# A batched attention-times-value product: from a scheduled tile program to hand-written engine programs with a register loop on TensorE

## The chip, the cores and the metric

One core of one Trainium2 chip. The metric is the device time of one launch in microseconds (us). Most runs of one kernel agree within 0.1% here. A "span" is the time from the first to the last instruction in the trace, 1.7 to 1.9 us less than the time (in e5 2.5 to 2.8 us). A transfer "lands" when its last piece has arrived, by the trace's semaphore records. Engines: PE is TensorE's matmul, PEld its weight load, DVE is VectorE, ACT ScalarE, POOL GpSimd, SP the sync engine.

## The reference

```python
batch, n_heads, seq, head_dim = 8, 12, 1024, 64
def reference(attn_weights, v):          # (8,12,1024,1024) and (8,12,1024,64), float32
    return np.einsum('bhqs,bhsd->bhqd', attn_weights, v).astype(np.float32)
```

There is no softmax: 403 MB of weights are read once, and every element is used in one product with 64 columns. Heads are taken two at a time, 48 "pairs" of 8 MB each; a pair is worked in 16 blocks, each of 64 queries of both heads.

## The kernel before

It is written on a tile framework that orders instructions and places semaphores. GpSimd issues the weight loads, which cast float32 to bf16 on the way (427.8 MB read at HBM, 240.4 MB in packets). The weights arrive with the query on the partitions, so TensorE transposes them (two bf16 as one 32-bit word; 128x128 f32 in the timeline), DVE and ACT copy the transposed blocks from PSUM to SBUF, and TensorE multiplies. The last three pairs ("direct") use the transposed weights as the stationary operand, in groups of four blocks, and get by without a transpose back.

```python
    abf_pool = ctx.enter_context(tc.tile_pool(name="abf", bufs=2))   # 4 MB of weights each
    at_pool = ctx.enter_context(tc.tile_pool(name="at", bufs=2))
    vr_pool = ctx.enter_context(tc.tile_pool(name="vr", bufs=2))     # v, for two pairs
    ...
    def pair(ip):
        ...
        for g in range(G):
            transpose_g(abf, at, g)              # 16 x 4 transposes, then a copy each
        load_ahead(ip)                           # weights of pair ip+2 into the freed buffer
        for h in range(2):
            for half in range(2):
                multiply(at, vbf, po, h, half)
        to_sbuf(po, ot)
        if ip % 2 == 0 and ip // 2 + 1 < NV:
            spread_v(ip // 2 + 1)                # v of the NEXT two pairs onto all partitions
        for j0 in (0, 4):
            last = transpose_back(ot, o_halves, j0, 4)
        if ip < NP - 1 - HELD:                   # HELD = 7: the last outputs are kept back
            store(ip, osb)
        else:
            held[ip] = osb
    ...
    def load_ahead(ip):
        nxt = ip + 2
        if nxt < NP:
            if nxt % 2 == 1 and (nxt + 1) // 2 < NV:
                load_v((nxt + 1) // 2)           # v of pairs nxt+1 and nxt+2
            last = load_attn(nxt)
            if nxt == NP - 1:
                ...                              # the held stores, behind the last load
```

## Time and profile before

| | before |
|---|---|
| time, median (range) | 1061.45 us (1061.05 to 1061.7, 4 runs) |
| span | 1059.6 us |
| DMA share, 100 to 900 us | 1.01 to 1.02 |
| PE busy / TensorE clock granted | 76% / 0.855 |
| instruction packets on the DMA engines | 44 of 16 KB |

The row to read first is the DMA share, the busy time of the core's 16 DMA engines. At 1.01 to 1.02 I read the idle time of the other engines (PE's 4.3 and 5.0 us ahead of two pairs in the prediction's timeline) as free: only work of the DMA engines, and the two ends of the run, should change the time. The lines themselves stand in the prediction.

### The profile page before, as it was taken

Reading aid. Unit: us, or ns where it says so; the run is one execution under the profiler, and the core shown is the slowest. Engines: PE = TensorE matmul, PEld = TensorE weight load, DVE = VectorE, ACT = ScalarE, POOL = GpSimd, SP = SyncE. Lnnn points to the kernel's source line nnn. Section 1 sums busy time; section 2 is a strip of 40 time slices with the busy share of each in tenths; the row PEclk is TensorE's granted clock in tenths of the full one; section 3 lists DMA queues with packets and bytes.
Section 4 is the critical chain, followed back from the end, with each engine's and each line's share of the span. In section 5 each row is a group of like instructions: output and inputs, shape, how many; then the busy total and the mean of one; then the engine's idle time right before and its main releaser. Section 6 shows DMA issues by size and latency. Waiting matters only on the chain.

```text
span 1059.6 us, 12899 instructions
## 1 busy us (share of the span) xinstructions
PE 808.4 (76%) x5640; PEld 645.0 (61%) x5640; DVE 390.7 (37%) x590; ACT 399.6 (38%) x486; POOL 71.8 (7%) x137
## 2 busy tenths in 40 slices
PE   0988778876778767787687876888678776788996
PEld 0676567654666556665476655766557555676785
DVE  0443334433344333343334333343334333344443
ACT  0353334433344333344344333443334333343542
POOL 2000000000000000000000000000000000001011
PEclk9998878988888888788888887788889887788999
DMA  9999999999999999999999999999999999999998
GB/s 217 219 218 234 222 237 231 225 226 222 239 224 232 222 231 237 223 220 231 238 226 229 227 224 236 229 222 229 229 230 235 221 227 228 236 215 210 217 215 243
DMA packets 19208, 240.43 MB, mean 227 GB/s; under 512 B 2128, under 2 KB 2512, under 8 KB 11984
## 3 DMA queue, kind: packets, MB, share of 16 engines
q0 software_dynamic: 18432, 238.03, 100.0%
q1 hardware_dynamic: 720, 1.57, 0.4%
q8 instruction: 44, 0.72, 0.2%
q14 instruction: 12, 0.10, 0.0%
HBM read 427.82 MB, written 25.17 MB: 428 GB/s over the span
## 4 chain that ended last, share of the span: by engine, by line
DMA 73%; issue 14%; PE 9%; POOL 2%; ACT 1%; DVE 0%; POOLq 0%
DMA abf<-in_attn_weights_dram 73%; PE pt L150 5%; PE px L186 2%; ACT osb L194 1%; POOL vr L124 1%; POOL out_dram L203 1%; PE px L136 1%; PE px L252 1%; PE po L169 0%; DVE vbf L144 0%; POOL abf L108 0%; DVE at L159 0%; ACT at L159 0%; DVE osb L263 0%; ACT osb L263 0%
## 5 line engine op out<-in xcount | busy, mean ns | idle before, releaser
L150 PE MATMUL pt<-ident,abf 128*128 128x128 f32 x3072 | 463.2, 319 | 194.3 <-DMA abf<-in_attn_weights_dram 194.3
L150 PEld LDWEIGHTS pt<-ident,abf 128*128 128x128 f32 x3072 | 449.7, 214 | 209.4 <-issue 116.3
L159 DVE COPY at<-pt 128x1024 bf16<-128x1024 bf16 x480 | 319.5, 688 | 443.1 <-PE pt L150 441.7
L159 ACT COPY at<-pt 128x1024 bf16<-128x1024 bf16 x288 | 288.7, 1012 | 223.3 <-PE pt L150 129.2
L169 PE MATMUL po<-at,vbf 128*64 128x512 bf16 x1440 | 216.5, 391 | 0.0
L169 PEld LDWEIGHTS <-vbf 128*64 128x64 bf16 x1440 | 106.5, 108 | 92.9
L194 ACT COPY osb<-px 128x512 f32<-128x512 f32 x90 | 50.8, 587 | 154.9 <-PE px L186 151.5
L181 ACT COPY ot<-po 128x512 f32<-128x512 f32 x45 | 26.3, 585 | 191.4 <-PE po L169 191.4
L186 PE MATMUL px<-ident,ot 128*128 128x128 f32 x360 | 69.8, 340 | 30.3 <-DVE vbf L144 17.4
L186 PEld LDWEIGHTS px<-ident,ot 128*128 128x128 f32 x360 | 52.8, 174 | 50.7 <-DVE vbf L144 28.7
L144 DVE CAST vbf<-px 128x512 bf16<-128x512 f32 x48 | 33.2, 691 | 95.9 <-PE px L136 95.9
L181 DVE COPY ot<-po 128x512 f32<-128x512 f32 x45 | 31.1, 691 | 100.8 <-PE po L169 100.8
L136 PE MATMUL px<-vr,spread 32*128 32x512 bf16 x384 | 53.8, 386 | 18.5 <-DVE vbf L144 18.5
L108 POOL DMA_DIRECT2D abf<-in_attn_weights_dram x58 | 31.5, 546 | 512.5 <-PE pt L150 507.2
L203 POOL DMA_DIRECT2D out_dram<-osb x47 | 25.2, 536 | 462.8 <-ACT osb L194 424.8
L144 ACT CAST vbf<-px 128x512 bf16<-128x512 f32 x48 | 28.1, 585 | 63.7 <-PE px L136 63.7
L136 PEld LDWEIGHTS <-spread 32*128 32x128 bf16 x384 | 17.2, 93 | 52.5 <-issue 43.0
L252 PE MATMUL px<-vbf,at 128*128 128x128 bf16 x384 | 23.9, 219 | 2.3 <-ACT at L159 1.2
L252 PEld LDWEIGHTS <-at 128*128 128x128 bf16 x384 | 22.5, 98 | 3.1 <-DVE at L159 1.5
L263 ACT COPY osb<-px 64x256 f32<-64x256 f32 (+2 forms) x14 | 4.7, 337 | 20.6 <-DVE osb L263 20.6
L124 POOL DMA_DIRECT2D vr<-in_v_dram x23 | 12.4, 538 | 0.0
L263 DVE COPY osb<-px 64x256 f32<-64x256 f32 (+2 forms) x14 | 5.3, 378 | 18.4 <-PE px L252 18.4
(10 smaller groups left out, 6.1 us busy)
## 6 DMA issues: line engine op xcount, KB each, us to landing
abf<-in_attn_weights_dram POOLq DMA_DIRECT2D x44, 4096.0 KB, 33.2
out_dram<-osb POOLq DMA_DIRECT2D x47, 512.0 KB, 20.0
vr<-in_v_dram POOLq DMA_DIRECT2D x23, 512.0 KB, 21.4
abf<-in_attn_weights_dram POOLq DMA_DIRECT2D x4, 2048.0 KB, 25.6
abf<-in_attn_weights_dram POOLq DMA_DIRECT2D x7, 1024.0 KB, 27.3
v<-in_v_dram SPq DMA_DIRECT2D x1, 1024.0 KB, 4.7
abf<-in_attn_weights_dram POOLq DMA_DIRECT2D x1, 512.0 KB, 29.7
abf<-in_attn_weights_dram POOLq DMA_DIRECT2D x2, 256.0 KB, 30.1
```

Source lines behind the costliest of these rows:

```text
L108: last = nc.gpsimd.dma_start(out=abf[:, ds(g0, gn)].rearrange("p g s -> p (g s)"), in_=attn_p[ip][:, ds(g0 * S, gn * S)],)
L124: nc.gpsimd.dma_start(out=vr.rearrange("p b x -> p (b x)"), in_=v_g[iv])
L136: nc.tensor.matmul(out=px, lhsT=spread[rows, b], rhs=vr[rows, b], start=(b == 0), stop=(b == VB - 1),)
L144: copy(out=vbf[:, :, h % 2], in_=px.rearrange("p (k d) -> p k d", k=SB))
L150: nc.tensor.matmul(out=pt[:, k], lhsT=words[:, k], rhs=ident, is_transpose=True, start=(k == 0), stop=(k == KW - 1),)
L159: copy(out=at[:, g].rearrange("c k j two -> c (k j two)"), in_=pt.rearrange("c k j -> c (k j)").bitcast(bf16),)
L169: nc.tensor.matmul(out=po[h][ds(half * D, D)], lhsT=vbf[:, 2 * kw + par, h], rhs=at[:, ds(half * GH, GH), kw, ds(h * HP, HP), par], start= ...
L181: copy(out=ot[:, :, h], in_=po[h].rearrange("p (j q) -> p j q", j=GH))
L186: last = nc.tensor.matmul(out=px[:, j], lhsT=ot[:, j0 + j].rearrange("p h q -> p (h q)"), rhs=ident, is_transpose=True, start=(j == 0), st ...
L194: nc.scalar.copy(out=o_halves[:, :, ds(j0, jn)].rearrange("p half j d -> p j half d"), in_=px.rearrange("p j (half d) -> p j half d", half=2),
L203: nc.gpsimd.dma_start(out=out_p[ip].rearrange("p g d -> p (g d)"), in_=osb.rearrange("p g d -> p (g d)"), single_packet=True,)
L252: behind = nc.tensor.matmul(out=px[:, g - g0].rearrange("p h d -> p (h d)"), lhsT=at[:, g, kw, :, par], rhs=vbf[:, 2 * kw + par].rearrange ...
```

## The change

The intent is to drop the framework's scheduling: one program per engine with its own semaphores, a loop on TensorE so that its program is short, and the transposes back of a pair moved behind the transposes of the next pair so that TensorE needn't wait for the copies. Core of the diff (about 650 lines; cuts marked):

```diff
-    at_pool = ctx.enter_context(tc.tile_pool(name="at", bufs=2))
-    vr_pool = ctx.enter_context(tc.tile_pool(name="vr", bufs=2))
-    HELD = 7
+    HELD = 9
+    with tc.tile_critical(no_gpsimd_drain=True):
+        at = sb("at", [P, G, KW, P, 2], bf16)                 # one, not two
+        vr = sb("vr", [P, VB, SB * D], bf16)
+        vr_last = sb("vr_last", [P, VB, SB * D], bf16)        # the last block of v alone
...
+        def pe_pair(i, n, before, waits, wait_v, first=False):
+            for g in range(G):
+                if g in waits:
+                    pe.wait_ge(*waits[g])
+                if g >= 4:
+                    pe.wait_ge(s_cp[i][g - 4], n)
+                transpose_g(abf[i], g)
...
+            spread_v(i, vr)                  # this pair's v, no longer the next one's
+            if not first:
+                transpose_back()             # of the pair before
...
+            multiply(i)
+        def pe_direct(p):
...
+                transpose_g(abf[i], g)
+                if g == 3:
...
+                    elif p == NP - 2:
+                        pe.wait_ge(s_vlast, 16)
+                    spread_v(i, vr_of(p))
...
+        with nc.Fori(1, LOOPED // 2, 1, engines=(PE,)) as it:
+            n = pe.snap(it + 1)
+            loaded = pe.snap(it * 16)
+            twice = pe.snap(loaded + 16)
+            pe_pair(0, n, it, {0: (s_abf[0], twice)}, (s_v, loaded))
+            pe_pair(1, n, n, {0: (s_abf[1], twice)}, None)
...
+        for p in range(NP - 2):              # GpSimd
+            pool.wait_ge(s_t[True], (p + 1) * PER_DVE)
+            if p % 2 == 1 and (p + 1) // 2 < NV:
+                iv = (p + 1) // 2
+                if iv < NV - 1:
+                    pool.wait_ge(s_sp[1], p + 1)
+                load_v(iv)
+            load_attn(p + 2)
+            if 0 < p <= HELD_FROM:
+                store(p - 1)
+        for p in range(HELD_FROM, NP - 1):
+            store(p)
```

## The prediction

> **What bounds the kernel now.** I read the busy shares first, then the DMA queues, the chain of work that ended last, and single stretches. From the page of the kernel before:
>
> ```profile
> PE 808.4 (76%) x5640; PEld 645.0 (61%) x5640; DVE 390.7 (37%) x590; ACT 399.6 (38%) x486; POOL 71.8 (7%) x137
> DMA  9999999999999999999999999999999999999998
> q0 software_dynamic: 18432, 238.03, 100.0%
> q8 instruction: 44, 0.72, 0.2%
> HBM read 427.82 MB, written 25.17 MB: 428 GB/s over the span
> DMA 73%; issue 14%; PE 9%; POOL 2%; ACT 1%; DVE 0%; POOLq 0%
> ```
>
> No compute engine is full, but the DMA row is nine in 39 of 40 slices, and the software queue alone fills the time of all 16 DMA engines. The chain is mostly DMA, by line the load of the attention weights (73%). The table of stretches says the same more finely (columns: stretch, its length, busy us and count of PE, PEld, DVE, ACT, POOL, granted clock, DMA share, GB/s):
>
> ```profile
> 300.00:500.00 200.00, 154.93 (x1027) 122.15 (x1024) 73.87 (x110) 75.39 (x91) 12.21 (x23) 0.82 1.02 229
> 500.00:700.00 200.00, 153.31 (x1019) 120.70 (x1017) 72.50 (x109) 75.54 (x92) 11.68 (x22) 0.84 1.01 228
> 1040.00:1050.00 10.00, 8.78 (x111) 8.12 (x109) 4.64 (x9) 3.72 (x6) 1.59 (x3) 1.00 1.03 335
> 1050.00:1060.00 10.00, 1.81 (x21) 1.42 (x20) 1.12 (x3) 1.54 (x4) 0.00 (x0) 0.79 0.41 160
> ```
>
> The share is 1.01 to 1.02 (packets overlap a little) up to the last 10 us. So the question for any change is only whether it alters the work of the DMA engines, or lets their queue run dry. The timeline around one pair answers the second (start, duration, engine, line, operation):
>
> ```profile
> 506.70 9.24 PE L150 MATMUL pt<-ident,abf 128*128 128x128 f32 x64 [4.33 <-DMA abf<-in_attn_weights_dram]
> 515.88 4.81 PE L169 MATMUL po<-at,vbf 128*64 128x512 bf16 x32
> 516.24 0.53 POOL L108 DMA_DIRECT2D abf<-in_attn_weights_dram  x1 [12.36 <-PE pt L150]
> 529.65 0.20 PEld L150 LDWEIGHTS pt<-ident,abf 128*128 128x128 f32 x1 [5.00 <-DMA abf<-in_attn_weights_dram]
> ```
>
> The next load is issued at 516.24, when the 64 transposes have freed its buffer; the load already in the queue lands only at about 529.6. So **13.4 us of work are still queued** when more is added. PE waits 4 to 5 us per pair for data, and that wait costs nothing. A pair takes 21.8 us.
>
> **The small thing that is left.** The chain in order of time gives one landing for every second pair:
>
> ```profile
> 178.69 0.70 PE pt L150 x2
> 222.33 0.70 PE pt L150 x2
> 266.97 0.49 PE pt L150
> 310.57 0.49 PE pt L150
> ```
>
> Steps: 43.64, 44.64, 43.60. Over the whole chain every step is 43.6 except four of about 44.65 (ending at 266.97, 442.45, 661.53, 880.60), 1.05 more. Two pairs move 16.78 MB of weights, 1.05 MB of v and 1.05 MB of output, 18.87 MB. The queue line above has 44 instruction packets, 0.72 MB, 16 KB each. This is TensorE's program: 11,280 instructions (5640 matmuls, 5640 weight loads) of 64 bytes are 0.72 MB. In the trace's list of single packets each fetch takes 0.89 to 0.97 us of one DMA engine, and the durations repeat with a period of eight fetches. In each of the four long steps lies a fetch of the first of these eight classes (0.893 us, or 892), and the long steps lie 4 or 5 double pairs apart, about eight fetches. My reading: fetches go round the DMA engines, and **only the one that falls on the slowest engine delays the landings, by 1.05 us**.
>
> [...] 18.87 MB in 43.6 us are 433 GB/s[...]. No loop is in the kernel before[...]. [...]
>
> **The change part by part.**
>
> (1) Traffic of data: the same loads with the same pieces, the same 4 MB per pair, the same v and output bytes, two weight buffers as before. 0 us.
>
> (2) TensorE's loop: pairs 2 to 43 come from 21 rounds of a body of two pairs. What is left in the program is 2 pairs ahead, 2 in the body, 1 after, 3 direct. A pair has 64 transposes, 16 spreads, 8 transposes back, 32 multiplications: 120 matmuls, 240 instructions; with some 18 waits as instructions of their own 258. A direct pair has 64 + 16 + 128 = 208 matmuls, about 456 with its waits. 5 x 258 + 3 x 456 = 2658 instructions are 10.4, so 11 blocks of 256 instead of 44. The body, 516 instructions, is about 33 KB[...]; I take it that it stays. 33 fetches fewer, one in eight on the slowest engine, 1.05 us each: **minus 4.3 us**.
>
> (3) One branch and a few register operations per round[...], on PE, beside 13.4 us of slack. 0 us.
>
> (4) Own semaphores: the waits on PE become about 18 per pair. Even at 0.2 us exposed for each of the 12 before transposes, the next load would be issued 2.4 us later, and 11 us would still be queued. 0 us. One copy of `at` instead of two, and the spread and transposes back between transposes and multiplication: PE's pair, in the stretches above 16.8 us of a 21.8 us pair (154 of 200 us busy), has the same work in another order; in-order issue makes the single buffer safe without a new wait ahead of the next pair's transposes other than those of the copies. The buffer of the weights still comes free after the transposes, which now come first in a pair as before. 0 us. The load of v waits for one spread in every second pair, some 2 us, ahead of the weights' load: inside the slack.
>
> (5) The end: 9 held stores instead of 7 lie behind the last loads, so the last piece lands some 2.5 us earlier (a 512 KB store at 433 GB/s is 1.2 us), and the last transposes no longer wait for the products before them. But the packets show 4 KB store packets to the very end, on engines that lag the fastest by up to 10 us; the engine that ends last has its whole share to do in any order. The end of the compute chain comes earlier by 2 to 4 us and is covered by stores: 0 us, at best minus 1.
>
> (6) The start: entering one critical section may add a barrier ahead of the first load, which is issued at 1.26 us now, and as the DMA is the bound, that would count fully. Plus 0.4 us, a guess.
>
> Sum: 1061.36 - 4.3 + 0.4 = 1057.5 us.
>
> **The rivals.** (a) *The loop refetches its body each round.* Then 21 rounds x 2 to 3 blocks plus the rest give 60 to 75 fetches, 15 to 30 more than now: plus 2 to 4 us if spread the same way, 1064 to 1066. [...] (b) *TensorE becomes the bound*, since waits on registers are slow or the serial order (transposes, spread, back, wait for the cast, multiply) leaves gaps. PE would need over 13 us more per pair between a landing and its last transpose before the queue dries, or over 21.8 us of work per pair in all, some 5 us more than now; beyond that, each us per pair costs 47 us of span. For it: PE at 76% is the next in line. Against: the 4 to 5 us waits for data. Then 1085 or more. (c) *The scheduling itself was costing much*, as the author's effort suggests: the 14% "issue" and 116 us of PE's weight load waiting on issue would come back. Against: those lie beside a DMA share of 1.01[...]. (d) *Fetches do not matter at all* and the long steps have another cause: 1061.5.
>
> **Range and chances.** The centre is (2) with (6). Below, a better end and every fetch counting give some 1053; above, rival (a) or (d) with a costlier start gives 1062. Faster by over 2% means under 1040[...]: 1%. Slower by over 2% needs rival (b): 3%. Within 2%: 96%.
>
> **What would show it.** Right: instruction packets near 11 on that queue; DMA share still 1.01 in the middle; landings every 43.6 us with at most one or two long steps; PE's wait for the weights still some us in each pair, DVE and ACT busy unchanged. Part (5): PE's last matmul comes earlier against the end, with stores filling the rest. Wrong: 60 or more fetches (rival a); a DMA share under 0.98 in the middle, or landings over 45 us apart with PE waiting on copies or semaphores (rival b); steps below 43.3 us (rival c); 11 fetches but the same long steps (rival d); a first load issued later than 2 us.

Cut from the recorded text are figures and rules that no run of this case shows, and what was argued from them. The sum came to 1057.5 us (1061.36, minus 4.3 of part (2), plus 0.4 of part (6)), and no number of it is cut; only the 0 us of part (3) has lost its ground, the author's estimate for a branch (measured later: 0.21 us in the changed kernel). That the loop's body stays was not shown by the kernel before. Two figures have their ground in the page: 64 bytes an instruction is the 0.72 MB of fetches over 11,280 instructions, and 256 to a block is a packet of 16 KB in such instructions. That TensorE issues in order is seen in the changed kernel, where it stands for 9.16 us at one transfer with weights at hand. The 0.2 us of part (4) and the 0.4 us of part (6) were suppositions; from the landing of a pair's weights to the next load's issue the changed kernel takes 9.8 us and not 9.5, and its first load is issued 0.2 us later.

## The result, and the profile after

| | before | changed |
|---|---|---|
| time, median (range) | 1061.45 us (1061.05 to 1061.7) | 1067.75 us (1067.52 to 1068.05) |
| span | 1059.6 us | 1066.0 us |
| instruction packets | 44 | 9 |
| last weights landed | 1048.6 us | 1041.0 us |
| last output landed | 1058.0 us | 1059.7 us |
| from there to the end of the span | 1.5 us | 6.3 us |

The ratio is 1.006 (interval 1.0042 to 1.0077): the same within 2%, but 6.3 us slower, where 4 us less was predicted, and outside the range. The last three rows come from the trace's records of each transfer's landing. Now the lines of the page that answer to those shown of before:

```profile
PE 792.5 (74%) x5640; PEld 635.4 (60%) x5640; DVE 391.8 (37%) x589; ACT 397.1 (37%) x485; POOL 71.1 (7%) x137
DMA  9999999999999999999999999999999999999994
q0 software_dynamic: 18432, 238.03, 99.3%
q8 instruction: 9, 0.15, 0.0%
HBM read 427.82 MB, written 25.17 MB: 425 GB/s over the span
DMA 67%; PE 29%; issue 1%; POOL 1%; ACT 1%; DVE 0%; POOLq 0%; SPq 0%
```

The bytes are the same and the engines are as busy. The instruction packets fell from 44 to 9. What is new is the last digit of the DMA row, a 4 where an 8 stood: the last 2.5% of the span are no longer filled with transfers. Next the landings of every second pair, from the chain in order of time (start, duration, what):

```profile
218.84 9.36 PE bank L129 x64
262.43 9.66 PE bank L129 x64
306.10 9.96 PE bank L129 x64
349.67 10.32 PE bank L129 x64
```

Steps of 43.59, 43.67 and 43.57, and none of the 44.65 steps of before anywhere in the chain. At pair 41 the changed kernel is ahead: the transposes of that pair start at 916.66 us, those of before at 924.22. So the body of the kernel did at least what was predicted, and the loss lies in the last 60 us. The timeline of one pair in the middle shows that the queue did not run dry either:

```profile
500.98 9.46 PE L129 MATMUL bank<-ident,abf 128*128 128x128 f32 x64 [3.93 <-DMA abf<-in_attn_weights_dram]
510.74 0.53 POOL L381 DMA_DIRECT2D abf<-in_attn_weights_dram  x1 [16.87 <-PE bank L129]
524.05 10.22 PE L129 MATMUL bank<-ident,abf 128*128 128x128 f32 x64 [6.86 <-DMA abf<-in_attn_weights_dram]
```

The next load is issued at 510.74 and the one in the queue lands at 524.0: 13.3 us of work queued, as before (13.4). Now the end, in the table of stretches (columns as in the prediction):

```profile
1010.00:1020.00 10.00, 1.75 (x15) 1.55 (x13) 1.60 (x3) 2.15 (x3) 7.35 (x14) 0.70 1.04 215
1040.00:1050.00 10.00, 9.07 (x108) 8.13 (x107) 4.99 (x9) 4.37 (x7) 0.54 (x1) 1.00 1.01 407
1050.00:1060.00 10.00, 7.47 (x92) 6.90 (x91) 4.25 (x8) 3.92 (x6) 0.00 (x0) 1.00 0.20 71
1060.00:1066.00 6.00, 0.00 (x0) 0.00 (x0) 0.00 (x0) 0.00 (x0) 0.00 (x0) 0.65 0.00 0
```

Two things: from 1010 to 1020 PE is busy for 1.75 us of 10 while the DMA engines are full, and from 1050 to 1060 it is PE that works while the DMA engines idle at 0.20. The order is turned round: the products are late and the transfers are done. And then 6 us with nothing at all. The timeline names the first, and the waits of the sync engine the second:

```profile
1008.65 0.53 POOL L387 DMA_DIRECT2D vr_last<-in_v_dram  x1 [23.64 <-PE bank L129]
1020.91 1.89 PE L144 MATMUL bank<-vr_last,spread 32*128 32x512 bf16 x8 [9.16 <-DMA vr_last<-in_v_dram]
1057.72 0.28 DVE L307 COPY osb<-bank 64x128 f32<-64x128 f32 x1 [0.53 <-PE bank L225]
```

```profile
SPq L447 <- ACT osb L307: 1055.3, 4, 1048.5
SPq L480 <- PEq L480: 5.6, 2, 4.6
SPq L454 <- DMA out_dram<-osb: 0.9, 1, 0.9
```

**First loss.** The last block of v is issued at 1008.65, behind all of pair 46's weights in the same queue, and lands at 1020.86. In a direct pair TensorE wants it after the first four blocks (`g == 3` in the diff) and does nothing further down its program before it has it: it stands still for 9.2 us with weights already in SBUF. After that it has two whole direct pairs to do, some 18 us each, and ends at 1057.7, long after the last store of GpSimd has landed (1052.2); the last three of the sync engine's four small stores run alone.

**Second loss.** The 4.6 us wait at the exit (line 480) is put down to "PEq", whose barrier signal this view saw last. The trace's record of the single instructions corrects it: PE's signal is given at 1060.04, and it is GpSimd's drain, from 1060.01 for 4.71 us, that everyone waits for. In the kernel before GpSimd also has such a drain, of 11.69 us from 1047.1, but there it starts right behind its last store and runs beside the tail; it ends 0.9 us behind GpSimd's last landing. Here GpSimd leaves the critical section together with the other engines, so its drain starts only 0.36 us behind the last landing of all (0.42 us in e1), and takes 4.71 us each time. A small part of the longer exit is something else: clearing the semaphores there takes 0.50 us and not 0.14.

### The profile page after: what moved, and what is told of

Its sections match the earlier page's. It is cut to its first block, busy times and chain, and to the rows that moved or that the text cites. A ratio compares the mean times of both kernels' runs of the same rounds, so it can differ in the third digit from the quotient of the medians.

```text
span 1066.0 us, 12832 instructions
## 1 busy us (share of the span) xinstructions
PE 792.5 (74%) x5640; PEld 635.4 (60%) x5640; DVE 391.8 (37%) x589; ACT 397.1 (37%) x485; POOL 71.1 (7%) x137
## 4 chain that ended last, share of the span: by engine, by line
DMA 67%; PE 29%; issue 1%; POOL 1%; ACT 1%; DVE 0%; POOLq 0%; SPq 0%
DMA abf<-in_attn_weights_dram 66%; PE bank L129 23%; PE bank L144 2%; PE bank L225 2%; DMA vr_last<-in_v_dram 1%; POOL vr L387 1%; PE bank L172 1%; ACT at L320 0%; PE bank L156 0%; DVE vbf L295 0%; DVE at L320 0%; DVE osb L307 0%; ACT osb L347 0%; ACT vbf L295 0%; POOL abf L381 0%
## 5 line engine op out<-in xcount | busy, mean ns | idle before, releaser
L129 PE MATMUL bank<-ident,abf 128*128 128x128 f32 x3072 | 464.1, 322 | 251.0 <-DMA abf<-in_attn_weights_dram 251.0
L129 PEld LDWEIGHTS bank<-ident,abf 128*128 128x128 f32 x3072 | 452.1, 215 | 273.3 <-DMA abf<-in_attn_weights_dram 247.7
L320 DVE COPY at<-bank 128x1024 bf16<-128x1024 bf16 x480 | 320.6, 689 | 469.8 <-PE bank L129 465.1
L320 ACT COPY at<-bank 128x1024 bf16<-128x1024 bf16 x288 | 289.0, 1012 | 421.5 <-PE bank L129 421.4
L172 PE MATMUL bank<-at,vbf 128*64 128x512 bf16 x1440 | 216.4, 391 | 0.8 <-DVE vbf L295 0.8
L172 PEld LDWEIGHTS bank<-at,vbf 128*64 128x64 bf16 x1440 | 106.5, 108 | 96.1 <-DVE vbf L295 8.2
L156 PEld LDWEIGHTS bank<-ident,ot 128*128 128x128 f32 x360 | 38.5, 140 | 19.1 <-issue 19.1
L156 PE MATMUL bank<-ident,ot 128*128 128x128 f32 x360 | 49.1, 280 | 0.0
L347 ACT COPY osb<-bank 128x512 f32<-128x512 f32 x90 | 48.3, 589 | 0.4
L144 PE MATMUL bank<-vr,spread 32*128 32x512 bf16 x368 | 48.1, 377 | 0.0
```

The source lines that it names most:

```text
L129: last = pe.matmul(out=pt[g % 4][:, k], lhsT=words[:, k], rhs=ident, is_transpose=True, start=(k == 0), stop=(k == KW - 1),)
L144: last = pe.matmul(out=po[h], lhsT=spread[rows, b], rhs=source[rows, b], start=(b == 0), stop=(b == VB - 1),)
L156: last = pe.matmul(out=px[n][:, ds(j * P, P)], lhsT=ot[:, 4 * n + j].rearrange("p h q -> p (h q)"), rhs=ident, is_transpose=True, start=(j ...
L172: last = pe.matmul(out=po[h][ds(half * D, D)], lhsT=vbf[i][:, 2 * kw + par, h], rhs=at[:, ds(half * GH, GH), kw, ds(h * HP, HP), par], sta ...
L320: ins = copy(out=at[:, g].rearrange("c k j two -> c (k j two)"), in_=bank[g % 4].bitcast(bf16),)
L347: last = nc.scalar.copy(out=halves[:, :, ds(4 * n, 4)].rearrange("p half j d -> p j half d"), in_=px[n].rearrange("p (j half d) -> p j hal ...
```

## The experiments

All ran correct. The four of the first group shared their runs of the kernel before (median 1061.49), the second group (e5 to e8) had 1061.67, the last (e9) 1061.38. The second group ran on another chip than the others, and a difference of 0.3 us between groups means nothing.

### e1: the last block of v one pair earlier

```diff
+            if p == NP - 4:
+                load_v(NV - 1)
-            if p % 2 == 1 and (p + 1) // 2 < NV:
+            if p % 2 == 1 and (p + 1) // 2 < NV - 1:
```

> The changed kernel with the last block of v loaded one pair earlier, ahead of pair 46's weights and not behind them. Theory (two losses at the end: TensorE stalled 9.2 us on that block and then has 37 us of products left, and a 4.7 us drain of GpSimd alone at the end): the 9.2 us wait goes, TensorE's last product ends near 1046 us instead of 1057.7, the end of the last store is then set by the held stores, whose last landing was 1052.2, and the time falls by 6 to 7 us, to about 1061. Rival (the late product is covered by the stores, only the drain counts): no change, 1067.7.

Measured: 1062.15 us (ratio to before 1.0005, 0.999 to 1.002), 5.6 us less than the changed kernel. TensorE's 9.2 us wait is gone; the last copy behind the last products comes at

```profile
1045.81 0.28 DVE osb L307
```

which is 11.9 us sooner, and the last store lands at 1054.04, not 1059.65. The end is again set by the stores: the pieces of the last one arrive between 1050.7 and 1054.04, and that limits the gain to 5.6 us where 6 to 7 were expected. (The DMA share of 1050 to 1060 is 0.17 here too. The sign of the late products was thus not the low share in itself, but that PE was still at work.) The rival falls.

### e2: a drain behind GpSimd's last store

```diff
         for p in range(HELD_FROM, NP - 1):
             store(p)
+        pool.drain()
```

> The changed kernel with one more drain on GpSimd, right behind its last store inside the critical section, where it runs while the products of the last pair are still being made. Theory: the drain at the end shrinks from 4.7 us to well under 1 us and the time falls by 4 to 5 us, to about 1063. Rival (the drain at the end has a fixed cost, whatever ran before): no change, 1067.7, or a little longer.

Measured: 1063.57 us, 4.2 us less than the changed kernel. The exit's wait, on what is now line 481, was 5.6 us with 4.6 the longest:

```profile
SPq L481 <- PEq L481: 1.1, 2, 0.9
```

The final drain's own record shrinks from 4.71 to 0.05 us; the added one runs from 1040.6 for 13.8 us beside the tail. The stretch from the last landing to the end falls from 6.3 to 1.9 us. So the rival falls: the drain has no fixed cost at the end; it only stood where nothing covers it.

### e3: both edits

> Both edits. Theory: they add up, because one acts ahead of the last store and the other behind it: about 1056 to 1057, some 5 us under the kernel before, which is what the prediction had worked out for the body of the kernel. Rival (one hides the other): no better than the better of the two, 1061.

Measured: 1059.89 us (ratio 0.9983, 0.997 to 0.9997), 7.9 us less than the changed kernel and under the kernel before, but some 3 us more than expected. With the products on time, the end comes so early that the added drain is not yet over: the last store lands at 1054.04, the drain ends at 1056.4, 2.4 us behind it, and all wait. The edits add up except for some 2 us (5.6 and 4.2 would make 9.8); the expectation had overlooked that the added drain ends only behind GpSimd's own last landing. The rival falls as well: 1059.89 us is better than either edit alone (1062.15 and 1063.57).

### e4: the loop on TensorE written out

```diff
-        with nc.Fori(1, LOOPED // 2, 1, engines=(PE,)) as it:
-            n = pe.snap(it + 1)
...
+        for it in range(1, LOOPED // 2):
+            n = it + 1
```

> The changed kernel with TensorE's loop written out (constants in place of registers), nothing else. Theory (instruction fetches cost landings): some 44 instruction packets instead of 9, four or five long steps of 44.65 us per double pair return, the landings fall behind those of the changed kernel by 4 to 6 us before pair 44. The time rises by about as much, 1072. Rival (the lead of 7.6 us at pair 42 comes from the order of transposes and loads, or from one queue position of v): landings as in the changed kernel, 1067.7.

Measured: 1072.91 us, 5.2 us more than the changed kernel (ratio to before 1.0106). The queue of instructions and three landings from the chain:

```profile
q8 instruction: 44, 0.72, 0.2%
```

```profile
219.04 9.45 PE bank L129 x64
263.56 9.39 PE bank L129 x64
307.33 9.66 PE bank L129 x64
```

Steps of 44.52 and 43.77. Over the whole chain four steps between 44.5 and 44.7 are back, as in the kernel before. The second half of pair 45's weights lands at 1003.31 us, against 998.92 in the changed kernel: **4.39 us for 35 fetches**. (The trace is of e4's slowest run, 1073.8 us. Before, it landed at 1007.70. The other 4.4 us of the changed kernel's lead are thus not the fetches. Most of it is work put off and not saved: two more stores held back and the last block of v not yet loaded, three transfers of about 1.25 us; e3 and e7 show the stores, below.)

Why only some fetches cost anything can be seen in the landings. The trace has 16 arrivals for each load, as many as there are DMA engines. In the kernel before, the time from the first to the last arrival of one load is 1.9 us at pair 9, and behind the four long steps it is 3.0, 4.1, 5.1 and 6.2 us. In e4 it grows in the same way, from 2.2 to 6.5 us; in the changed kernel it stays at 2.0 to 2.3 us up to pair 39. So the fetches put some of the engines further and further behind, and a load has landed only when the last one is through.

### e5 and e6: how large the loop's body may be

```diff
-        with nc.Fori(1, LOOPED // 2, 1, engines=(PE,)) as it:
+        with nc.Fori(0, (LOOPED // 2 - 1) // U, 1, engines=(PE,)) as r:     # on top of e3
+            for u in range(U):                                              # U = 7 in e5, 3 in e6
+                it = pe.snap(r * U + (1 + u))
```

> Both edits as in e3, with 14 pairs in the loop's body and 3 rounds, some 3600 instructions[...]. Theory ([...]a body that doesn't fit is fetched again each round): 40 or more instruction packets, the landings late by 4 to 5 us again as in the unrolled kernel, about 1064. Rival (any loop, or the register waits, give the gain): 9 to 15 packets and the time of e3, 1059.9.

> Both edits as in e3, with 6 pairs in the body and 7 rounds, some 1550 instructions[...]. Theory: about 13 to 14 instruction packets, one more of them at most on the slowest DMA engine, 1060 to 1061. Rival (only a body of two blocks is kept and larger ones are fetched again): over 40 packets and about 1064.

Measured: e5 1066.12 us, e6 1059.45 us, against 1059.89 of e3. First e5, then e6:

```profile
q8 instruction: 49, 0.80, 0.3%
```

```profile
q8 instruction: 12, 0.20, 0.1%
```

A body of 6 pairs is fetched once; by the trace it has 1364 instructions (not 1550), 87 KB at 64 bytes each (the 0.72 MB of the kernel before over its 11,280 instructions). One of 14 pairs (3180, not 3600; 204 KB) is fetched again in each round, the long steps are back, and the last store lands at 1059.9 and not 1054.0. The trace's list of single instructions shows the refetch directly: the two branches back to the start of the body take 7.26 us each in e5, and 0.21 to 0.24 us in e6, e3 and the changed kernel. The next load is issued 7.4 us later than in e3 (387.55 against 380.15), which is inside the 13.3 us that are queued. The two blocks of e6's rival are what the changed kernel's body fills (454 instructions, 29 KB); 87 KB stay as well, so it falls. The runs show only that 87 KB stay and 204 KB do not. The loop and its register waits as such gain nothing (e5 has both and takes 6.2 us more than e3): what counts is whether the body is fetched again, 49 packets against 12. The expectation for e5 was 2 us low: the chain has five long steps (44.66 to 44.79 us) and not four, the last landing came 5.8 us later than in e3, and 0.7 us or more lie outside the span. e6 came out a little under its 1060 to 1061.

### e7: seven stores held back, not nine

```diff
-    HELD = 9
+    HELD = 7          # on top of e3
```

> Both edits as in e3, with 7 stores held back instead of 9. Theory (the DMA work is the same and its end is set by the slowest DMA engine): the last weights land some 2.5 us later, at about 1043.4 and not 1040.9, the last store still lands near 1054, the time stays within 1 us of e3. Rival (the two more stores held are worth their 2.5 us): 1062.

Measured: 1058.83 us, 1.1 us less than e3. The second half of pair 45 lands 2.56 us later than in e3 (1001.39 against 998.84), the last weights at 1043.4, the last store at 1053.8: holding more stores back moves work, and saves none; the rival (1062) falls. The 1.1 us come from the exit (the drain ends at 1055.7 here).

### e8 and e9: the last stores on another queue

```diff
-        for p in range(HELD_FROM, NP - 1):
+        for p in range(HELD_FROM, NP - 4):       # e9: NP - 6
             store(p)
         pool.drain()
...
+                if k == 1:                       # on the sync engine, in its loop of last stores
+                    for p in range(NP - 4, NP - 1):
+                        store(p, nc.sync)        # counted with the other last stores
```

> Both edits as in e3, and the last three held stores issued on the sync engine's queue once the last pair's first group is out, so that GpSimd's last transfer lands earlier and its drain can end before the last store. Theory (in e3 the drain ends 2.4 us behind GpSimd's last landing and holds the end by about 2 us): the drain is over by the time the last store lands near 1054, the time falls by 1.5 to 2.5 us to about 1057.7. Rival (the drain does not hold the end, or the stores on a second queue take longer): 1060 or more.

> As e8, with five of the held stores on the sync engine's queue and four left on GpSimd's. In e8 the two queues shared the DMA engines, so GpSimd's six stores still landed as late as 1053.7 and its drain ended 2.3 us behind that. Theory (the drain follows GpSimd's last landing by 2.0 to 2.4 us): with four stores on GpSimd its last landing comes near 1051.5, the drain ends by 1053.9, before the last store on the other queue (about 1054.2), and the time falls by another 1 to 2 us against e8, to 1057 to 1058. Rival (the drain's end is set by something else, such as its own start): no change from e8, 1059.1.

The moved stores also go without `single_packet`, which was not tested by itself. Measured: e8 1059.08 us, only 0.8 us less than e3, about half of the least that was expected. With both queues at work the last of GpSimd's six stores still landed at 1053.66, and its drain ended 2.2 us behind that. With five stores moved (e9) GpSimd's last store lands at 1049.1, well before the sync queue's last one at 1054.11, the added drain ends at 1051.3, again 2.2 us behind GpSimd's last landing, the final one takes 0.05 us, and the time is **1057.70 us** (1057.2 to 1057.95; ratio to before 0.9963, 0.995 to 0.9977). This version beats both kernels. It goes beyond the change, since it moves stores to another queue.

## Why the prediction was wrong

**What held.** That the DMA engines bound the kernel (a share of 1.01 to 1.02 from 100 to 900 us in both); that the loop would take the fetches from 44 to about 11 (9); that the body of the loop stays and is not fetched each round (rival a falls: in the changed kernel no fetch stands between 92 and 982 us, and e6 has 12 in all); that PE doesn't become the bound in the middle (rival b: 13.3 us still queued); and about the size of the gain from fewer fetches: minus 4.3 us predicted, 4.4 us of landings measured by e4 and 5.9 by e5. Rival (d), that fetches do not matter, falls with e4 and e5.

**The step that failed first** is part (4), "The load of v waits for one spread in every second pair, some 2 us, ahead of the weights' load: inside the slack." It asked when the transfer is issued and not what stands before it in the queue, nor where in its program TensorE asks for it. In the looped pairs the spread stands behind all 16 blocks, and each v lands 2.4 to 3.8 us behind its pair's weights, while the 16 blocks take some 10 us: hidden, as assumed. In direct pair 46 it stands behind the fourth block, while v stands behind all of that pair's weights. With it fell part (5), "The end of the compute chain comes earlier by 2 to 4 us and is covered by stores: 0 us, at best minus 1." The chain ended 4 us later. Cost: 5.6 us (e1).

**The second** is part (6): it priced entering the critical section ("plus 0.4 us, a guess") and forgot leaving it. Entering cost 0.2 us (the first load is issued at 1.48 and not 1.26). Leaving puts GpSimd's drain behind everything: the stretch from the last landing to the end grew from 1.5 to 6.3 us, 4.8 us. An early drain (e2) brings it to 1.9 us; the longer clearing of the semaphores makes up the rest.

The sum closes on the spans. From before to e3, with both repairs, the last landing moves from 1058.04 to 1054.04, minus 4.0 (fetches minus 4.4, start plus 0.2, and 0.2 that I can't place). The late block of v brings it to 1059.65, plus 5.6. The exit adds 4.8. Together plus 6.4, and the spans are 1059.6 and 1066.0. With both losses out of the way, e9 stands at 1057.7 us, where the prediction had put the change itself (1057.5), but that is a coincidence: e9 has five stores on another queue as well.

**Sums and readings of the prediction that don't hold,** though the result doesn't hang on them. A pair has 8 spreads and not 16 (x384 for 48 pairs in the page), and few waits are instructions of their own: by the trace 227 instructions a looped pair and not 258, 409 to 423 a direct one and not 456. That is 9.2 blocks of 256 and not 10.4, and 9 were measured; that the gain still came out near minus 4.3 us is luck in a small way. Part (3): a branch back takes 0.21 us; beside the 13.3 us of slack no cost shows, the steps stay at 43.57 to 43.67 us. The 433 GB/s count bytes at HBM; with the cast the packets bring only 228 to 229 GB/s in the stretches, and no run shows which of the two is at a limit, so a lower limit to the time isn't shown either. And the "up to 10 us" by which engines lag is 8.4 us at most between the arrivals of one transfer.

**What stays open.** Why GpSimd's drain takes 4.71 us when nothing is left to wait for, and why it ends 2.0 to 2.4 us behind its last landing in e2, e3 and e5 to e9 but 0.9 us in the kernel before. That fetches put some DMA engines behind the others is shown by the arrivals (e4); which engine takes which fetch is not, since the trace does not name the engine of a packet, and that the long steps go with one class of fetches out of eight stays a pattern.

## What to carry to other kernels

When the DMA engines are full (here a share of 1.01 to 1.02), look at each transfer's place in the queue and at the place in the consumer's program that waits for it. Here a small transfer behind a large one, wanted before the large one was used up, held TensorE for 9.2 us, and near the end, where nothing covered it, that cost 5.6 us (e1). Price both ends of a new synchronisation scope: a drain that ran beside the tail for 11.69 us in the kernel before ended up behind it, for 4.71 us. And holding stores back, or loading later, made the middle of a trace look faster without saving anything (two more stores held: pair 45's weights 2.56 us sooner in e3 than in e7, the time no shorter), so compare the last landing as well.
